# Products of h before the scan, Winograd values and queries, and a scan of four heads at once

## The chip, the cores and the metric

One core of one Trainium2 chip runs the kernel. The metric is the device time of one execution in microseconds, lower is better. The kernel before was run three times: 1786.86, 1792.22 and 1791.27 us, median 1791.27 us.

## The reference, cut to what matters

One residual block on 1024 tokens of 1024 features, all in float32. The part that the change touches is the gated linear attention of branch A:

```python
h = rms_norm(x, pre_mix_norm)
proj = h @ w_in        # q 4x128, k 4x128, v 4x256, gate 4x256, decay 16, c_q 384, c_kv 256, k_pe 64
q = h_q * 128 ** -0.5
log_a = log_sigmoid(h_a @ w_a2 + b_a2) / 16
b = cumsum(log_a, over the 64 tokens of a chunk)
k_dec = k * exp(b_end - b)
def step(state, chunk):
    state = exp(b_end) * state + k_dec.T @ v      # 128 x 256 per head
    out = q @ state
o = rms_norm(o, gla_norm) * silu(h_g)
...
mixed = (g_a * (o @ w_o_gla) + g_b * (attention @ w_o_mla)) @ w_out
x = x + rms_norm(mixed)
x = x + rms_norm(swiglu(rms_norm(x)))
```

Branch B is latent attention of eight heads from c_q, c_kv and k_pe; its code is not changed.

## The kernel before, in words

Activations lie transposed, feature on partitions and token along the row, in eight feature tiles (k tiles) of 128 x 1024. Every float32 operand of a product is split into a high and a low part: ACT rounds the high part (L104, or an activation of its own), DVE subtracts it to give the low part (L105), and `mm3` (L96) issues three matmuls for one product. Many large products take the seven-product form of Strassen and Winograd on 2 x 2 blocks (function `wino`): blocks b11, b21, b22 of the activations and the sums t1 to t4, and sums s1 to s4 of the weights, give seven block products of 12 matmuls each per row block in place of eight. `early1` computes the two products on b11 and b21 before the other operands exist, keeps one of them in DRAM (p1D) and reads it back later; `HPRE` is the number of groups treated so.

The order of the work is the order in which the Python code emits it, with a scheduler of the framework moving instructions of one engine past each other. Generators of side work (`run`, `back`) are advanced a piece at a time. SP issues all DMAs.

- 0 to 52 us: each k tile of x arrives, is split, and 24 matmuls make keys from it (p_k, eight psum banks).
- 52 to 92 us: decay input and rotary key (p_ha), the norm, h = x * gain * 1/rms (L351) with both token halves of all eight tiles split (hn), the plain product of the first head's queries (p_q) and of one latent tile (p_c).
- 92 to 137 us: values of head 0 (`v_proj`, p_v, 256-column matmuls, hn x wv), with `decays()` between the pieces: per token tile, p_z (decay logits), three ACT functions and one DVE step (L395), p_rv and p_tot (sums over a chunk), exp, and the decayed key kF (L410). It ends with four transposes (p_decp).
- 137 to 366 us: for each of the four heads, `gla_scan(hd)` with the next head's values as fill (for the last head, early products p_pre). Decayed keys are masked to two zero-padded copies (kdm, even and odd chunk) and so are queries (qm), so that all matmuls span 128 rows. Per token tile the state is updated (p_kv, st L734), split (sh, sl) and multiplied with q (p_o); the output is normed (rpow on POOL, L176), transposed (p_oT) and stored (oD). `down_sums` (L622 to L625) makes the 48 sums of blocks of the down projection's weights here, on DVE.
- 366 to 582 us: the other products of the 14 groups on h (`hrest`, p_wa and p_wb): latents, branch gates, output gates; `og_use` multiplies the gate with oD and stores ogD. The latents' norms run beside them (`side`).
- 582 to 842 us: preparation and latent attention of eight heads; from 842 us merge, output product, feed-forward.

Of the kernel before, what the change touches and what calls it, by code (L numbers as in the profile page):

```python
# [23 lines left out]
P = 128  # L24
# [37 lines left out]
HPRE = 14  # L62


def body(tc, a, out):
# [89 lines left out]
    def back(n=1):  # L155
        """emit n pieces of background work"""
# [21 lines left out]
    def norm(sq, dim, box, want_tok=None):  # L178
        """sq [128, 512]: squares summed over feature tiles; box gets 1/rms on every partition."""
# [24 lines left out]
    oD = dp.tile([8, P, 1024], F32, name="oD")  # L204
# [8 lines left out]
    hnD = dp.tile([8, P, 1024], F32, name="hnD")  # L213
# [80 lines left out]
    for kt in range(KD):  # L294
# [26 lines left out]
        else:  # L321
            back()
    rtok = cp.tile([P, NT], F32, name="rtok")
# [8 lines left out]
    # ---- decay input and rotary key (rows 0-63: key, 64-79 and 96-111: decay input)  # L332
# [11 lines left out]
    back(10)  # L344

# [1 line left out]
    hn = []  # L347
    for kt in range(KD):
        t = xs[kt]
        for j in range(2):  # L350
            dve.scalar_tensor_tensor(t[:, HS[j]], t[:, HS[j]], g(G_PRE + kt), rb[j], op0=ALU.mult, op1=ALU.mult)  # L351
        hn.append([])
# [5 lines left out]
        if kt == 1:  # L358
            hsb = U([P, 2, H2], name="hsb")
            act.copy(hsb, hps)  # L360

    haS = U([P, 1024], F32R, "haS")
# [6 lines left out]
    dma(krD, kraw[0:64])  # L369
    act.activation(haS[64:128], hat[64:128], AF.Identity, bias=gn[64:128, G_ONE:G_ONE + 1])  # L370
# [10 lines left out]
    def decays():  # L381
# [3 lines left out]
        for t in range(NT + 1):  # L385
# [12 lines left out]
            if prev is not None:  # L398
                u, (ph, pl) = t - 1, prev
                # sums over the rest of a chunk, and over each chunk (rows 2u and 2u + 1)  # L400
# [9 lines left out]
                dve.scalar_tensor_tensor(kf, kf, rtok[:, u:u + 1], e, op0=ALU.mult, op1=ALU.mult)  # L410
# [11 lines left out]
    # Winograd's form of Strassen's product on 2 x 2 blocks (K halves, token halves, tile pairs):  # L422
    # seven block products in place of eight.  Block (i, k) of the result is tile i, token half k.
    def op4(srcs, name):
        """[128, 512] blocks -> operand parts"""
        res = []
        for s in srcs:
            hl = U([P, 2, H2], F32R, name)
            split(s, hl[:, 0], hl[:, 1])
            res.append((hl[:, 0], hl[:, 1]))  # L430
        return res
# [8 lines left out]
    def wino(ops, slot, groups, npre):  # L440
        """groups: (weights, first tile, second tile, consumer).  Two steps: early() gives the first npre
        groups' products on b11 and b21 piece by piece; rest(side) all others, with side() called between
        the products."""
# [19 lines left out]
        pend = []       # (operand, product) with the operand's split emitted  # L463
# [120 lines left out]
    def t_ops(ops, b11, b12, b21, b22):  # L584
        """the operands from differences, from the float32 blocks (overwritten) of one pair of k tiles"""
        t3 = Hf("t3")
        dve.tensor_tensor(t3, b22, b12, op=ALU.subtract)
        if len(ops["b22"]) < 4:
            ops["b22"] += op4([b22], "b22")
        yield 1  # L590
        dve.tensor_tensor(b12, b12, b11, op=ALU.subtract)      # T1 = B12 - B11
        dve.tensor_tensor(b22, b22, b12, op=ALU.subtract)      # T2 = B22 - T1
        ops["t2"] += op4([b22], "t2")
        ops["t3"] += op4([t3], "t3")
        ops["t1"] += op4([b12], "t1")
        dve.tensor_tensor(b21, b21, b22, op=ALU.subtract)      # -T4 = B21 - T2
        ops["t4"] += op4([b21], "t4")
        yield 1

# [15 lines left out]
    def down_sums():  # L615
        """the sums of blocks of the down projection's weights"""
        for p in range(4):
            for c in range(0, KH * P, H2):
# [3 lines left out]
                dve.tensor_tensor(a22, a21, a22, op=ALU.add)           # S1 = A21 + A22  # L622
                dve.tensor_tensor(a21, a11, a21, op=ALU.subtract)      # S3 = A11 - A21
                dve.tensor_tensor(a11, a22, a11, op=ALU.subtract)      # S2 = S1 - A11
                dve.tensor_tensor(a12, a12, a11, op=ALU.subtract)      # S4 = A12 - S2  # L625
# [33 lines left out]
    ws = [wload(a["wq"][0]), wload(a["wc"][2])]  # L659
    pss = [A(name="p_q"), A(name="p_c")]  # L660
    for kt in range(KD):
        for m in range(2):
            for j in range(2):
                mm3(pss[m][:, j], ws[m][kt], hn[kt][j], kt == 0, kt == KD - 1)
    for j in range(2):
        t = Hf("cr")
        act.copy(t, pss[1][:, j])  # L667
        dma(crD[2, j], t)
    run(dgen)

# [9 lines left out]
    # rotary key  # L680
# [824 lines left out]
```

## Time and profile before

| what | value |
|---|---|
| runs | 1786.86, 1792.22, 1791.27 us (median 1791.27) |
| span of the profiled execution, first to last instruction | 1789.7 us |
| PE busy | 1742.2 us |
| DVE busy | 1269.8 us |
| ACT busy | 811.3 us |
| POOL busy | 37.9 us |
| mean granted clock of PE | 0.993 |

The profiled execution is known by its span alone, 1.6 us under the median of the runs. PE's busy time is the union of its matmuls; matmuls overlap, so the time that one costs is the distance between two starts and not its own duration. A window of the profile gives the busy time of each engine between two times. Idle time of an engine counts only where another engine waits for it.

### The profile page before, as it was taken

How to read it: one execution, taken by the hardware profiler on the slowest of the kernel's cores; microseconds unless marked ns; L12 is line 12 of the kernel's file. 1: busy time of each engine (PE TensorE's matmuls, PEld its weight loads, DVE VectorE, ACT ScalarE, POOL GpSimd, SP SyncE). 2: the span in 40 equal slices, each digit the busy share in tenths (PEclk: the TensorE clock that was granted, in tenths of full speed). 3: DMA queues.
4: the chain of work that ended last, by engine and by line, in shares of the span. 5: the costliest groups of instructions: out<-in, count | busy, mean ns of one | idle time of the engine just before them, and what ended most of it. 6: DMA issues, size and time to landing. Idle time of an engine off the chain costs nothing.

```text
span 1789.7 us, 25279 instructions
## 1 busy us (share of the span) xinstructions
PE 1742.2 (97%) x8818; PEld 1468.0 (82%) x8818; DVE 1269.8 (71%) x2275; ACT 811.3 (45%) x1511; POOL 37.9 (2%) x49
## 2 busy tenths in 40 slices
PE   8999999999999999999999999999999999999997
PEld 7889997777778898998878788787877788878886
DVE  7666666765766787787697567687787866755666
ACT  5485545633434554555442545452322233454552
POOL 0100000000000000000000000000000000000001
PEclk9999999999999999999999999999999999999998
DMA  6326676865576211112588653645454532593656
GB/s 213 129 80 197 192 235 223 276 200 184 195 238 222 67 45 49 35 51 95 169 302 284 207 191 129 240 140 177 165 183 141 182 101 97 182 312 116 195 176 215
DMA packets 172592, 305.50 MB, mean 171 GB/s; under 512 B 20080, under 2 KB 39280, under 8 KB 172464
## 3 DMA queue, kind: packets, MB, share of 16 engines
q1 hardware_dynamic: 172464, 303.88, 51.6%
q8 instruction: 69, 1.13, 0.3%
q14 instruction: 59, 0.48, 0.1%
HBM read 212.32 MB, written 89.39 MB: 169 GB/s over the span
## 4 chain that ended last, share of the span: by engine, by line
PE 74%; DMA 10%; DVE 9%; issue 3%; ACT 3%; SPq 1%; POOL 0%; DVEq 0%; ACTq 0%; POOLq 0%
PE p_wb L96 13%; PE p_wfd L96 10%; PE p_wa L96 9%; PE p_pre L96 6%; PE p_v L96 5%; PE p_wog L96 5%; PE p_wout L96 5%; PE p_sc L96 4%; PE p_av L96 3%; PE p_k L96 3%; DMA raw<-in_wfg_dram 2%; PE p_wqn L96 2%; DMA raw<-in_wgate_dram 1%; PE p_pt L1013 1%; DMA cl<-crD 1%
## 5 line engine op out<-in xcount | busy, mean ns | idle before, releaser
L104 ACT CAST wh<-raw 128x512 fp32r<-128x512 f32 (+1 forms) x335 | 200.2, 603 | 367.2 <-PE p_wfd L96 79.7
L105 DVE TENSOR_TENSOR wl<-raw,wh 128x512 fp32r<-128x512 f32 (+1 forms) x335 | 219.7, 663 | 153.8 <-ACT wh L104 142.8
L96 PE MATMUL p_wa<-t,wh 128*128 128x512 f32 x640 | 203.1, 397 | 5.0 <-DVE u L520 4.8
L96 PE MATMUL p_wb<-t,wh 128*128 128x512 f32 x640 | 198.1, 390 | 0.0
L96 PE MATMUL p_wfd<-ld,wh 128*128 128x512 f32 (+1 forms) x660 | 192.8, 376 | 2.3 <-ACT raw L1411 1.4
L96 PEld LDWEIGHTS p_wa<-t,wh 128*128 128x128 f32 x640 | 119.9, 190 | 35.5 <-DVE u L520 9.9
L96 PEld LDWEIGHTS p_wfd<-ld,wh 128*128 128x128 f32 x660 | 120.7, 188 | 26.1 <-ACT raw L1411 1.8
L96 PEld LDWEIGHTS p_wb<-t,wh 128*128 128x128 f32 x640 | 120.5, 188 | 25.1
L96 PE MATMUL p_wa<-t,wl 128*128 128x512 f32 x320 | 125.3, 393 | 0.0
L96 PE MATMUL p_wb<-t,wl 128*128 128x512 f32 x320 | 124.5, 389 | 0.0
L96 PE MATMUL p_wfd<-ld,wl 128*128 128x512 f32 (+1 forms) x330 | 123.1, 375 | 0.0
L104 ACT CAST wh<-sa 128x512 fp32r<-128x512 f32 x80 | 48.6, 620 | 149.3 <-DVE sa L458 90.4
L96 PE MATMUL p_v<-wh,hn 128*128 128x256 f32 x512 | 98.2, 283 | 0.7 <-ACT cr L667 0.6
L104 ACT CAST wh<-sb 128x512 fp32r<-128x512 f32 x80 | 49.7, 621 | 92.7 <-PE p_wb L96 47.5
L96 PEld LDWEIGHTS p_v<-wh,hn 128*128 128x128 f32 x512 | 82.3, 191 | 3.5 <-ACT cr L667 1.0
L96 PE MATMUL p_wog<-ld,wh 128*128 128x512 f32 x256 | 80.4, 392 | 1.0 <-DVE ld L105 0.7
L96 PE MATMUL p_pre<-b,wh 128*128 128x512 f32 x256 | 79.3, 396 | 0.0
L105 DVE TENSOR_TENSOR ld<-ld,ld 128x512 fp32r<-128x512 f32 x109 | 70.5, 686 | 11.3 <-ACT ld L104 10.9
L104 ACT CAST ld<-ld 128x512 fp32r<-128x512 f32 x109 | 63.5, 619 | 22.2 <-DMA ld<-fD 7.6
L96 PE MATMUL p_v<-wl,hn 128*128 128x256 f32 x256 | 72.4, 283 | 0.5 <-DVE wl L105 0.5
L96 PEld LDWEIGHTS p_wa<-t,wl 128*128 128x128 f32 x320 | 60.8, 190 | 13.1
L96 PEld LDWEIGHTS p_wfd<-ld,wl 128*128 128x128 f32 x330 | 62.1, 188 | 11.2
(349 smaller groups left out, 4076.4 us busy)
## 6 DMA issues: line engine op xcount, KB each, us to landing
ld<-fD SPq DMA_DIRECT2D x77, 256.0 KB, 4.1
raw<-in_wfd_dram SPq DMA_DIRECT2D x60, 256.0 KB, 2.8
raw<-in_wfg_dram SPq DMA_DIRECT2D x60, 256.0 KB, 3.6
raw<-in_wfu_dram SPq DMA_DIRECT2D x60, 256.0 KB, 3.0
raw<-in_wgate_dram SPq DMA_DIRECT2D x48, 256.0 KB, 3.3
fD<-sg SPq DMA_DIRECT2D x41, 256.0 KB, 2.0
p1D<-p SPq DMA_DIRECT2D x34, 256.0 KB, 3.0
p<-p1D SPq DMA_DIRECT2D x34, 256.0 KB, 3.9
```

The costliest lines, as they stand in the source:

```text
L96: pe.matmul(o, l, r, start=start, stop=stop, skip_group_check=skip)
L104: act.copy(h, src)
L105: dve.tensor_tensor(l, src, h.bitcast(F32), op=ALU.subtract)
L1013: pe.transpose(tp[:, jj, i * P:(i + 1) * P], prs[i][:, j * P:(j + 1) * P], ident)
```

## The change

- Values of all heads are made before the scan, in the seven-product form with 512-column matmuls (`v_gen`), and stored to DRAM (vD). The sums of the weights' blocks are made by POOL (`v_sums`, 16 operations of 128 x 512) while the keys are computed, from 16 loads of wv, and stored (svD).
- Queries of all heads are two more groups of `wino`, stored to qD; the output gates are stored as sgD and multiplied in the scan. `HPRE` falls from 14 to 6, the groups rise from 14 to 16.
- The latent tile p_c is computed from the split x right after p_ha and scaled later. The first query product is gone.
- h: only the first token half of each tile is split (hb); the second half goes straight into the sums t1 to t4 (`h_ops`, `t_ops`), with two of the four sums (t3 and b21) on POOL. The store and reload of h (hnD, `spilled_ops`) go.
- Decayed keys are split once (ACT kh, POOL kl) and stored to kdD, eight times.
- The scan runs after `hrest`, all four heads together: for each token tile two steps (a pair of heads each). An update is a matmul of 64 rows (the chunk's own tokens) in place of 128 zero-padded rows. The low part of the state is one 128 x 1024 operation per step, on DVE for the first pair and on POOL for the second (8 each). The preparation of the first attention heads (`pair_prep(0)`) is its fill.
- `down_sums` moves to POOL and is advanced during attention.

```diff
-HPRE = 14
+HPRE = 6
+        if kt >= 2:
+            run(vsum)
...
-        for j in range(2):
-            hl = U([P, 2, H2], F32R, "hn")
-            split(t[:, HS[j]], hl[:, 0], hl[:, 1])
-            hn[kt].append((hl[:, 0], hl[:, 1]))
-        dma(hnD[kt], t)
+    def t_ops(ops, b11, b12, b21, b22, alt=dve):
+        t3 = Hf("t3")
+        alt.tensor_tensor(t3, b22, b12, op=ALU.subtract)
...
+        dve.tensor_tensor(b12, b12, b11, op=ALU.subtract)
+        dve.tensor_tensor(b22, b22, b12, op=ALU.subtract)
...
+        alt.tensor_tensor(b21, b21, b22, op=ALU.subtract)
...
-                dve.scalar_tensor_tensor(kf, kf, rtok[:, u:u + 1], e, op0=ALU.mult, op1=ALU.mult)
+                dve.scalar_tensor_tensor(e, kf, rtok[:, u:u + 1], e, op0=ALU.mult, op1=ALU.mult)
+                kh, kl = Hf("kh", F32R), Hf("kl", F32R)
+                act.copy(kh, e)
+                pool.tensor_tensor(kl, e, kh.bitcast(F32), op=ALU.subtract)
+                dma(kdD[0, u], kh.bitcast(F32))
+                dma(kdD[1, u], kl.bitcast(F32))
...
-                dve.tensor_tensor(a22, a21, a22, op=ALU.add)           # S1 = A21 + A22
+                pool.tensor_tensor(a22, a21, a22, op=ALU.add)
...
+    vgen = v_gen()
+    for _ in range(9):
+        run(vgen)
         run(dgen)
-    for _ in range(4):
-        run(hpre)
+        run(hgen)
+    for _ in hpre:
+        run(hgen)
         run(dgen)
...
+                    for e in range(2):
+                        rsl = slice(64 * e, 64 * e + 64)
+                        mm(kv[:, e, hh], kd[t][x][rsl, hd * P:(hd + 1) * P], v[t][y][rsl, hd * DV:(hd + 1) * DV], n == 0, n == 2)
...
+            act.copy(sh, s2)
+            (pool if pr else dve).tensor_tensor(sl, s2, sh.bitcast(F32), op=ALU.subtract)
...
+    fill = pair_prep(0)
+    for n, _ in enumerate(gla_scan()):
+        if n >= 3:
+            run(fill)
```

The order of SP's queue in the first stage. Before, loads alone (x of one k tile, then weights):

```order
L298 DMA x_225<-in_xT_dram 128x1024
L110 DMA raw_694<-in_wq_dram 128x512
L110 DMA raw_700<-in_wc_dram 128x512
L110 DMA raw_706<-in_wc_dram 128x512
L298 DMA x_276<-in_xT_dram 128x1024
```

Now (x_236 and x_295 are the fourth and fifth k tile, vs the blocks of the values' weights):

```order
L323 DMA x_236<-in_xT_dram 128x1024
L309 DMA svD<-vs_231 128x512
L309 DMA svD<-vs_228 128x512
L309 DMA svD<-vs_230 128x512
L309 DMA svD<-vs_229 128x512
L323 DMA x_295<-in_xT_dram 128x1024
```

Four stores of sums that POOL makes now stand ahead of a load of x; the same holds once more, ahead of the load of the seventh k tile.

The end of the decays on PE. Before, products of the values (p_v) stand between the decays' last steps and up to their transposes:

```order
L96 MATMUL p_v_1388<-wh_1378,hn_632 128x256
L96 MATMUL p_v_1613<-wh_1366,hn_597 128x256
L96 MATMUL p_v_1613<-wl_1367,hn_597 128x256
L96 MATMUL p_v_1613<-wh_1366,hn_597 128x256
L96 MATMUL p_v_1613<-wh_1366,hn_606 128x256
L96 MATMUL p_v_1613<-wl_1367,hn_606 128x256
L418 MATMUL p_decp_1254<-cst,tot_1248 128x16 x4
```

Now:

```order
L96 MATMUL p_v_784<-wh_1149,hb_780 128x512
L96 MATMUL p_rv_1131<-lh_1066,rev 128x512
L96 MATMUL p_tot_804<-lh_1066,rev 16x512
L96 MATMUL p_rv_1131<-ll_1067,rev 128x512
L96 MATMUL p_tot_804<-ll_1067,rev 16x512
L96 MATMUL p_z_1165<-wh_752,haS_731 128x512
L96 MATMUL p_z_1165<-wl_753,haS_731 128x512
L96 MATMUL p_rv_1179<-lh_1127,rev 128x512
```

The last of the values' first two products stands ahead of the last three decay steps, which follow each other with no product between, then the transposes, and behind them everything else.

POOL and DVE in the same stage, now. POOL (x_98 and x_295 are the first and the fifth k tile of h):

```order
L483 TENSOR_TENSOR kl_862<-e_858,kh_861 128x512
L394 TENSOR_TENSOR t_185_867<-x_295,x_98 128x512
L403 TENSOR_TENSOR x_295<-x_295 128x512
L483 TENSOR_TENSOR kl_913<-e_909,kh_912 128x512
L483 TENSOR_TENSOR kl_974<-e_970,kh_973 128x512
```

DVE:

```order
L480 SCALAR_TENSOR_TENSOR e_858<-kF_542,rtok,e_858 128x512
L398 TENSOR_TENSOR x_98<-x_98 128x512
L399 TENSOR_TENSOR x_295<-x_295,x_98 128x512
L105 TENSOR_TENSOR wl_1264<-raw_1253,wh_1263 128x512
L465 SCALAR_TENSOR_TENSOR h_895<-p_z_890,h_893 128x512
```

DVE's L398 overwrites a block that POOL's L394 reads, and L394 stands behind the low part kl of a key whose decayed form DVE has only just made (L480). Before, POOL had no work of this kind in the stage.

## Rows read from the trace of the kernel before

**Rows 1.** Page, part 1: busy time, share of the span, instructions per engine.
```profile
PE 1742.2 (97%) x8818; PEld 1468.0 (82%) x8818; DVE 1269.8 (71%) x2275; ACT 811.3 (45%) x1511; POOL 37.9 (2%) x49
```

**Rows 2.** Windows by stage: length, busy (instructions) of PE, PEld, DVE, ACT, POOL; clock; DMA.
```profile
69.50:91.00 21.50, 21.50 (x96) 17.65 (x95) 20.92 (x33) 12.59 (x21) 5.36 (x8) 1.00 0.52 183
...
92.00:137.50 45.50, 44.41 (x292) 38.77 (x293) 29.21 (x46) 34.54 (x63) 0.00 (x0) 1.00 0.28 87
137.50:366.00 228.50, 224.80 (x1445) 201.63 (x1444) 156.21 (x286) 124.60 (x273) 12.07 (x16) 1.00 0.68 224
366.00:582.00 216.00, 207.66 (x916) 169.29 (x916) 142.69 (x227) 86.94 (x137) 4.79 (x4) 0.98 0.63 207
598.00:842.00 244.00, 240.82 (x1528) 216.94 (x1526) 190.47 (x493) 129.56 (x285) 0.00 (x0) 1.00 0.16 49
```

**Rows 3.** Timeline of PE: start, us, form; 256 and 512 columns.
```profile
153.34 0.28 PE L96 MATMUL p_v<-wh,hn 128*128 128x256 f32 x1
153.46 0.28 PE L96 MATMUL p_v<-wl,hn 128*128 128x256 f32 x1
...
1442.66 0.62 PE L96 MATMUL p_wb<-b,wh 128*128 128x512 f32 x2
...
1443.34 0.39 PE L96 MATMUL p_wb<-b,wh 128*128 128x512 f32 x1
```

**Rows 4.** PE's groups by form: instructions, busy us, mean ns.
```profile
L96 PE MATMUL p_v<-wh,hn 128*128 128x256 f32 x512 | 98.2, 283 | 0.7 <-ACT cr L667 0.6 <-ACT wh L104 0.2
...
L96 PE MATMUL p_q<-hn,wh 128*128 128x512 f32 x128 | 40.3, 395 | 0.4 <-DVE vl L105 0.4
...
L96 PE MATMUL p_kv<-vh,kdm 128*128 128x256 f32 x128 | 28.7, 289 | 0.0
```

**Rows 5.** Timeline of PE: transposes of 16 rows, next product.
```profile
129.29 0.41 PE L418 MATMUL p_decp<-cst,tot 16*128 16x16 f32 x4
129.63 0.74 PE L96 MATMUL p_pre<-hn,wh 128*128 128x512 f32 x2
```

**Rows 6.** Waits of PE in 366 to 582 us: total, times, longest.
```profile
PE p_wa L96 <- DVE u L520: 3.4, 2, 2.9
PE p_nrm L96 <- DVE cl L643: 2.9, 2, 2.2
```

**Rows 7.** Windows: first and last of three stretches of lower clock; one late product group.
```profile
378.00:382.00 4.00, 4.00 (x16) 3.16 (x15) 1.51 (x3) 0.62 (x1) 0.00 (x0) 0.81 0.61 196
510.00:514.00 4.00, 4.00 (x13) 3.14 (x12) 2.58 (x5) 1.34 (x2) 0.00 (x0) 0.67 0.70 242
1444.19:1463.45 19.26, 19.26 (x85) 15.69 (x85) 15.15 (x24) 6.49 (x12) 0.00 (x0) 1.00 0.46 151
```

**Rows 8.** POOL's groups by form.
```profile
L1400 POOL TENSOR_TENSOR raw<-raw,xr 128x256 f32<-128x256 f32 x6 | 4.4, 730 | 10.3 <-DVE raw L1399 8.5 <-DMA xr<-x1D 1.8
...
L714 POOL MEMSET kdm<- 64x1024 f32 x2 | 1.9, 951 | 2.8 <-DMA hnD<-x 2.7
L716 POOL MEMSET qm<- 128x512 f32 x2 | 1.1, 530 | 3.5 <-DMA hnD<-x 2.3 <-DVE hn L105 1.2
```

**Rows 9.** Waits of ACT in 0 to 52 us.
```profile
ACT xh L305 <- DMA x<-in_xT_dram: 10.5, 8, 2.7
```

**Rows 10.** Timeline of DVE: scaling and split of h.
```profile
63.40 2.07 DVE L351 SCALAR_TENSOR_TENSOR x<-x,gn,rb 128x512 f32<-128x512 f32 x3
...
66.65 1.28 DVE L105 TENSOR_TENSOR hn<-x,hn 128x512 fp32r<-128x512 f32 x2
```

**Rows 11.** Timeline near the end, DVE with POOL idle, then both.
```profile
1783.95 0.41 DVE L1400 TENSOR_TENSOR raw<-raw,xr 128x256 f32<-128x256 f32 x1
...
1784.67 0.90 DVE L1400 TENSOR_TENSOR raw<-raw,xr 128x256 f32<-128x256 f32 x1
...
1784.57 0.72 POOL L1400 TENSOR_TENSOR raw<-raw,xr 128x256 f32<-128x256 f32 x1 [1.22 <-DMA xr<-x1D]
```

**Rows 12.** DVE's groups by form, state of the scan.
```profile
L734 DVE SCALAR_TENSOR_TENSOR st<-st,dec,p_kv 128x256 f32<-128x256 f32 x60 | 28.4, 474 | 9.0 <-PE p_kv L96 8.4
```

More of the change, by code (lines that the diff above doesn't have):

```diff
@@ L203, in body @@
     krD = dp.tile([64, 1024], F32, name="krD")
-    oD = dp.tile([8, P, 1024], F32, name="oD")
+    qD = dp.tile([HEADS_A, P, 1024], F32, name="qD")
+    kdD = dp.tile([2, NT, P, H2], F32, name="kdD")
+    vD = dp.tile([2, NT, P, 1024], F32, name="vD")
+    svD = dp.tile([4, 4, P, H2], F32, name="svD")
+    sgD = dp.tile([8, P, 1024], F32, name="sgD")
     ogD = dp.tile([8, P, 1024], F32, name="ogD")
@@ L658, in body @@
     dgen = decays()
[L659 to L669, printed above, removed]
     def rot_tables():
@@ L807, in body, with v_use, v_gen, halves @@
-    hops = dict(b11=[t[0] for t in hn[:4]], b21=[t[0] for t in hn[4:]], b22=[t[1] for t in hn[4:]],
-                t1=[], t2=[], t3=[], t4=[])
-    def lat_use(m0, m1):
+    def v_use(i, t, src):
+        h, l = Hf("vh", F32R), Hf("vl", F32R)
+        split(src, h, l)
+        for n, x in enumerate((h, l)):
+            dma(vD[n, 4 * (i % 2) + t][:, HS[i // 2]], x.bitcast(F32))
+    def v_gen():
+        def halves():
+            t = [U([P, 2, H2], name="vu") for _ in range(2)]
+            return [t[n // 2][:, n % 2] for n in range(4)]
+        def prod(src, bop, bank, first):
+            for k in range(4):
+                w = wop(wraw(src(k)))
+                for t in range(4):
+                    mm3(bank[t], cols(bop[k], slice(t * P, (t + 1) * P)), w, first and k == 0, k == 3, not first)
+                yield 1
+        def raw(i, j):
+            return lambda k: v_block(i, j, k)
+        def summed(n):
+            return lambda k: svD[n, k]
+        x = [A(name="p_v") for _ in range(2)]
+        x = [x[t // 2][:, t % 2] for t in range(4)]
+        yield from prod(raw(0, 0), hops["b11"], x, True)
+        p1 = halves()
+        for t in range(4):
+            act.copy(p1[t], x[t])
+        yield from prod(raw(0, 1), hops["b21"], x, False)
+        for t in range(4):
+            v_use(0, t, x[t])
+        yield 1
+        y = [B(name="p_v") for _ in range(4)]
+        u2 = halves()
+        yield from prod(summed(1), hops["t2"], y, True)
+        for t in range(4):
+            dve.tensor_tensor(u2[t], y[t], p1[t], op=ALU.add)
+        yield from prod(summed(2), hops["t3"], y, False)
+        for t in range(4):
+            dve.tensor_tensor(p1[t], y[t], p1[t], op=ALU.add)
+        yield from prod(summed(0), hops["t1"], x, True)
+        for t in range(4):
+            c = Hf("c22")
+            dve.tensor_tensor(c, x[t], p1[t], op=ALU.add)
+            v_use(3, t, c)
+        yield from prod(raw(1, 1), hops["t4"], y, True)
+        for t in range(4):
+            dve.tensor_tensor(p1[t], y[t], p1[t], op=ALU.add)
+            v_use(2, t, p1[t])
+        yield from prod(summed(3), hops["b22"], x, False)
+        for t in range(4):
+            dve.tensor_tensor(u2[t], x[t], u2[t], op=ALU.add)
+            v_use(1, t, u2[t])
+        yield 1
@@ L882, in body @@
-    back(100)
-    for _ in hpre:
-        finish(sgen)
-        run(ggen)
-    finish(ggen)
-    lgen = [x for i in range(2) for x in [latent_norm(i)]]
+    finish(vgen)
+    lgen = [latent_norm(i) for i in range(2)]
     def side(gi):
-        if gi >= 2 and gi % 2 == 0:
+        if gi >= 5 and lgen:
             while lgen and next(lgen[0], None) is None:
                 lgen.pop(0)
+        else:
+            back()
     hrest(side)
@@ new lines, in body, with gla_out @@
+    fill = pair_prep(0)
+    for n, _ in enumerate(gla_scan()):
+        if n >= 3:
+            run(fill)
+    finish(fill)
+    def gla_out(j, ogs, use):
+        for m in range(8):
+            w = wload(a["wog"][m])
+            ga = Hf("ga")
+            dma(ga, gaD[m][:, HS[j]])
+            ps = B(name="p_wog")
+            for kt in range(KD):
+                mm3(ps, w[kt], ogs[kt], kt == 0, kt == KD - 1)
+                if kt == 3:
+                    yield 1
+            dve.tensor_tensor(ga, ps, ga, op=ALU.mult)
+            use(m, ga)
+            yield 1
@@ L1049, in body @@
     gen = prep_all()
+    sums = down_sums()
     done = 0
@@ L1055, in body @@
             done = max(done, need[hd])
+        run(sums)
         cur = (hd, blk, qk(hd, blk))
```

330 lines of the change are left out of this document (154 added, 176 removed).

## Prediction

> **What bounds the kernel now.** The page's first part says PE: busy for 97% of the span, DVE for 71%, POOL for 2% [rows 1]. I therefore price each part of the change on PE first and then ask, stage by stage, whether DVE or POOL becomes the later one. The windows by stage show where there is slack [rows 2]: DVE is busy 29.2 of 45.5 us beside the decays, 156 of 228.5 in the scans, 143 of 216 in the rest of the products on h, 190 of 244 in attention; PE is idle only a few us in each. Busy PE is not PE at its pitch, so I compare with pitches: starts 0.12 us apart for 256 columns, and three matmuls of 512 columns in 0.68 us, 0.227 each [rows 3]. A change of less than 0.3% (5.4 us) can't be told from none here; with the median of 1791.3 "the same" is 1785.9 to 1796.7.
>
> **PE's savings.**
> Values: 512 + 256 matmuls of 256 columns [rows 4] at 0.12 are 92.2 us. The new form has 7 x 4 x 12 = 336 of 512 columns, 76.3 us: **-15.9**. Queries: 128 + 64 [rows 4] at 0.227 are 43.6; two groups of 84 are 38.1: **-5.5**. The latent tile costs the same in its new place.
> Updates: 128 + 64 of 256 columns [rows 4], 23 us. Two halves of 64 rows each can at best run side by side, which would save 11.5; at worst each costs what a full one did, 0. It counts only where PE bounds the scan, which I doubt below: **0**. The only row with few rows is four transposes of 16, and the next product begins 0.34 us after their start [rows 5]: 0.085 each, with 16 columns. It shows no stop of PE between the two forms.
> The scans' window: 942 matmuls of 256 columns at 0.12, 436 of 512 at 0.227 and 64 short ones at 0.11 make 219 us; it lasts 228.5 [rows 2], so 9.5 us go to small stalls where short products alternate. Products of h alone have few (about 2 for this content): **-7.4** (-9 to -5).
> The rest of the products on h: 852 matmuls of 512 columns and 64 short ones make 200.5 us; the window lasts 216 [rows 2], a loss of 15.5. PE waits for DVE [rows 6], and after each of three such waits its clock is low for a while: 4 us with 0.81 granted, later 4 us with 0.67 [rows 7], so part of it is spent at the lower of its two levels, 1.2 GHz. All 14 groups here have six products left and reload the seventh; a late group with all seven takes 19.26 us for 84 matmuls, 0.2 over its pitch [rows 7]. Of 16 groups now 10 are whole, and the latents' norms, which make one of those waits [rows 6], keep to later groups: loss 6 instead of 15.5, **-10** (-14 to -5).
>
> **What comes on top.**
> Keys: four stores of svD stand ahead of the fifth k tile's load in SP's queue, four more ahead of the seventh's. Each group waits for four additions on POOL. Price of one: POOL took 730 ns for 128 x 256 [rows 8]; its fills take 530 for 512 columns and 951 for 1024, so the fixed part is 0.11 and 512 columns should cost about 1.35 (between 0.73 and 1.46). Four are 5.4 us, just what 24 matmuls of one k tile last (5.45). ACT already waits for x in this stage, 10.5 us in all [rows 9], so a late x is late on PE. Bounds: 0, if POOL keeps up, and 2 x 5.4; I take the middle, **+5**.
>
> Decays: the stage that I think decides. DVE starts scaling at 63.40, at 0.665 us per piece and 0.61 per split [rows 10]. By the changed order, 90 DVE operations stand up to the last decayed key: 32 with a scalar, 57 without, one wide: 21.3 + 34.5 + 1.2 = 57.0 us. So DVE alone ends at 120.4. PE has p_ha, then p_c (the 96 matmuls of 69.5 to 91 us were p_q and p_c [rows 2]; p_c's 48 are 10.9 us, to 80.4), then 96 matmuls of the values' first two products and 48 of the decays, 32.7 us: it ends at 113.1. Behind it nothing but the last decay steps may run. That is 7 us of wait with DVE undisturbed. But POOL has 19 operations there (sums, kl, t3, b21), 25.7 us. The trace has one place where the two meet: a DVE addition of two SBUF operands takes 0.41 us alone and 0.90 when it starts 0.1 us into one of POOL's of 0.72, both ending within 0.3 us [rows 11]: DVE stood still until POOL was through. The Trainium skill ("SBUF — State Buffer", section "Who interferes with whom") states this as an exclusive lock for DVE instructions with two SBUF inputs beside a GpSimd instruction that reads SBUF; by it all 57 plain operations are exposed, and the trace's one meeting agrees. Besides, DVE's L398 must wait for POOL's t3, which stands behind a kl that waits for ACT: some 3 us each, four times. All of POOL's time in DVE's way would be +33, none of it +4 to +7. I take half of POOL's 25.7: **+20** (+4 to +30).
>
> Scan: DVE has 60 state updates of 474 ns [rows 12], 0.394 from start to start (neighbours overlap by some 0.08, as the three scalings of 0.74 that take 2.07 [rows 10]), 4 copies, 16 low parts of q, 32 gated outputs of the same size, 8 low parts of 1024 columns at 1.15, 26 preparation steps at 0.605, 16 tiny ones: 69.5 us. PE has 58 to 69 (updates 11.5 or 23, outputs 23, transposes 7, preparation 16). Before, this content lay under 219 us of other products. POOL has 8 low parts at 2.59 (a 1024-column price by the same line) and five groups of `down_sums`, 45 us; every second state waits for its low part on POOL, behind a group of sums of up to 5.4 us. DVE operations with two SBUF operands (50 of them) meet it half the time: about 12 us. With 3 us to fill the chain the scan ends after 84.5 against the 69.1 that the same matmuls cost before: **+15.5** (0 to +28).
>
> Attention: the rest of the sums on POOL, beside 78% of DVE busy [rows 2], PE waiting for DVE's operands already: **+3** (0 to +8). DVE loses 27 us of sums from the scans, where it was not the bound: 0. Stores and reloads (qD, vD, sgD, kdD instead of hnD, oD) lie in stages with DMA at 0.16 to 0.68 [rows 2]: 0, and if the reload of a tile comes late in the scan it is inside that range.
>
> **Sum.** -15.9 - 5.5 - 7.4 - 10 + 5 + 20 + 15.5 + 3 = +4.7 us, on a profiled span of 1789.7 (1.6 under the median of the runs): 1794.4, or **1796** as a median. The 38.8 us that PE saves are given back where POOL and DVE stand in one another's way.
>
> **Rivals.**
> *A: POOL's work falls into DVE's gaps.* DVE has a third of every stage free, and one meeting in the trace is little evidence. Then the decays cost +4 and the scan +3: 1796 - 16 - 12.5 = **1768**. It decides by the decays' transposes: before 125 us for A, after 135 for the forecast.
> *B: slower, the lock in full.* If each of POOL's operations stops DVE, and the low part of each second state waits behind a group of sums: keys +9, decays +30, scan +28, attention +8, together 31.5 over the forecast: **1827**. It decides from the point at which more than three quarters of POOL's time shows up as longer DVE operations.
> *C: the halves of 64 rows do not run side by side*, so that this part does not do what it says. The 16-row transposes speak for a price per matmul that few rows don't lower. Updates then cost 23 us: nothing while DVE bounds the scan; where PE bounds it, +11.5, **1806** with the rest as forecast. The Trainium skill ("TensorEngine Tiling (Array Packing)", section "Key Properties") says that a change of tiling mode drains TensorE; with 32 changes in the scan a stop would go on top, but the row of the transposes shows none of 0.1 us, so I add nothing.
>
> **How the numbers follow.** Forecast 0.44, its own range 1784 to 1808 (the decays at 13 or 27, the scan at 8 or 22); A 0.30 (1755 to 1782), because POOL's time is only 80 us in stages where DVE has some 180 free; B 0.20 (1812 to 1840); C as the deciding part 0.06. The range leaves out about the lower tenth (most of A's better half below 1760) and the upper tenth (B above 1824): **1760 to 1824**. Faster by over 0.3%: A and 0.04 of the forecast, 0.34. Same: 0.26, a good half of the forecast. Slower: the rest of it, B and C, 0.40.
>
> **What would show it.** Right: PE's matmuls fall by 456 (432 of the values, 24 of the queries); a gap on PE of 10 to 25 us in front of p_decp, put down to DVE or ACT steps of the decays; subtractions on DVE of 1 us and more where POOL is busy; a scan stage of 80 to 90 us with DVE over 80% busy; the rest of h at 0.23 us per matmul. Wrong: p_decp before 125 us; DVE's mean for a 128 x 512 subtraction still 0.69; a scan of 70 us with PE at its pitch; or a gap in the key stage of more than 10 us.

## The result, and the profile after

| | time |
|---|---|
| before, 4 runs | 1791.62 us median (1786.86 to 1792.22) |
| after, 4 runs | 1901.84 us median (1900.62 to 1904.92) |
| ratio | 1.0618, 95% interval 1.0596 to 1.0641 |

110 us slower; 1796 was forecast, with a range up to 1824. The profiled execution of the changed kernel has a span of 1898.6 us. The page's first part and its row of the granted clock, which answer to [rows 1]:

```profile
PE 1758.5 (93%) x8362; PEld 1451.3 (76%) x8362; DVE 1281.4 (67%) x2249; ACT 810.0 (43%) x1495; POOL 160.6 (8%) x133
...
PEclk9987999999976879999999999999999999999998
```

PE has 456 matmuls fewer, as the change says, and yet more busy time (1758.5 for 1742.2 us): in two stretches of the clock's row, the decays (slices 3 and 4) and the scan (12 to 15), the granted clock is below nine tenths. POOL went from 38 to 161 us.

To see where the 110 us lie, I cut both traces at the same events of PE: first p_v, p_decp, last product on h, end of the latent attention (last p_av). After (window, its length, then PE, PEld, DVE, ACT, POOL busy with instructions, clock, DMA share, GB/s; the third window ends at the scan's last transposes and the fourth goes on to the last p_av):

```profile
87.20:160.00 72.80, 41.68 (x146) 27.47 (x144) 50.15 (x75) 48.48 (x88) 17.52 (x14) 0.77 0.37 131
160.00:548.10 388.10, 377.74 (x1652) 306.53 (x1652) 222.37 (x345) 156.15 (x253) 16.98 (x15) 0.99 0.50 165
548.10:706.00 157.90, 99.64 (x558) 81.90 (x557) 79.74 (x166) 57.99 (x148) 60.59 (x48) 0.71 0.76 244
706.00:989.60 283.60, 278.16 (x1729) 248.73 (x1728) 219.47 (x544) 147.23 (x320) 24.92 (x20) 1.00 0.30 95
989.60:1898.60 909.00, 886.23 (x3965) 725.31 (x3963) 644.01 (x1037) 359.10 (x632) 12.37 (x13) 0.99 0.57 188
```

Before, with the scans inside the second window:

```profile
92.40:129.30 36.90, 36.21 (x255) 32.11 (x255) 23.98 (x37) 31.55 (x56) 0.00 (x0) 1.00 0.19 57
129.30:581.40 452.10, 440.06 (x2395) 377.06 (x2394) 303.64 (x520) 213.75 (x413) 16.86 (x20) 0.99 0.66 216
581.40:880.30 298.90, 295.00 (x1837) 264.72 (x1836) 231.56 (x574) 156.47 (x337) 0.00 (x0) 1.00 0.20 62
880.30:1789.70 909.40, 885.17 (x3965) 724.06 (x3963) 644.29 (x1037) 358.70 (x632) 11.95 (x13) 0.99 0.57 188
```

| stage | before | forecast | after |
|---|---|---|---|
| start to first p_v | 92.4 | 85.4 | 87.2 |
| first p_v to p_decp | 36.9 | 52.7 | 72.8 |
| p_decp to the last product on h | 452.1 | 377 | 388.1 |
| last product on h to last p_av | 298.9 | 370 | 441.5 |
| the rest | 909.4 | 909 | 909.0 |

The forecast column is the prediction's sum written by these events (p_c's end at 80.4 and the 5 us of the keys; for the products on h, what the other rows leave of 1794.4). Its error of 104 us has four parts: the start +2, decays +20, products on h +11, and the stage with the scan **+71**. The scan itself, 548 to 706 us, has PE busy for 99.6 of 157.9 us, and that at a clock of 0.71; DVE, which was to be its bound, is busy for half of it. So no engine's throughput sets it. What PE waits for there (total, times, longest):

```profile
PE p_o L96 <- ACT sh L970: 19.9, 14, 4.3
PE p_kv L96 <- DMA vh<-vD: 16.2, 3, 12.1
PE p_o L96 <- POOL sl L971: 5.5, 6, 1.8
PE p_kv L96 <- DVE st L966: 4.7, 4, 2.0
```

One step of the scan, all engines in order of time (start, duration, engine, line, operation, idle time before it and what ended that):

```profile
604.81 0.69 DVE L886 TENSOR_TENSOR qr<-p_qp,cos 128x512 f32<-128x512 f32 x1
605.42 0.47 DVE L966 SCALAR_TENSOR_TENSOR st<-st,dec,p_kv 128x256 f32<-128x256 f32 x1
...
605.80 0.68 DVE L887 TENSOR_TENSOR qr<-qr,qt 128x512 f32<-128x512 f32 x1
...
606.41 0.48 DVE L966 SCALAR_TENSOR_TENSOR st<-st,dec,p_kv 128x256 f32<-128x256 f32 x1
...
607.17 0.69 DVE L891 TENSOR_TENSOR ql<-qr,qs 128x512 fp32r<-128x512 f32 x1
...
608.57 0.99 DVE L966 SCALAR_TENSOR_TENSOR st<-st,dec,p_kv 128x256 f32<-128x256 f32 x2
...
609.59 1.04 ACT L970 CAST sh<-st 128x1024 fp32r<-128x1024 f32 x1 [2.45 <-DVE st L966]
...
610.69 0.58 PE L96 MATMUL p_o<-sh,qm 128*128 128x256 f32 x1 [4.30 <-ACT sh L970]
610.71 2.35 POOL L971 TENSOR_TENSOR sl<-st,sh 128x1024 fp32r<-128x1024 f32 x1 [10.40 <-ACT sh L970]
...
612.21 0.88 DVE L983 TENSOR_SCALAR ty<-ty 128x2 f32<-128x2 f32 x1
...
613.11 0.58 PE L96 MATMUL p_o<-sl,qm 128*128 128x256 f32 x1 [1.84 <-POOL sl L971]
...
613.16 0.70 POOL L176 TENSOR_TENSOR ty<-ty,mhalf 128x2 f32<-128x2 f32 x1
```

This is one round. DVE updates the state in four operations; a sum (L887), a copy and a split (L891) of the attention's preparation and two gated outputs stand between them, so the last two start 3.2 us after the first. ACT rounds the state (1.04), PE starts its output with the rounded part after 4.30 us of waiting; POOL needs 2.35 for the low part, PE waits 1.84 more. At 612.21 DVE's operation on 128 x 2 elements takes 0.88 us; the median of its 16 in the scan is 0.17. It ends with POOL's: DVE had to wait for POOL. Five of the 16 start well inside an operation of POOL's (598.79, 612.21, 636.60, 659.32 and 686.59 us); they take 0.35 to 0.88 us and all end within 0.03 us of it. The Trainium skill ("SBUF — State Buffer", section "Who interferes with whom") says that tensor_scalar can contend with GpSimd when its operands meet the conditions of a mode that uses both ports; this row agrees.

### The profile page after: what moved, and what is told of

Same layout as the page of the kernel before. It is cut to its first block, busy times and chain, and to the rows that moved or that the text cites. A ratio compares the mean times of both kernels' runs of the same rounds, so it can differ in the third digit from the quotient of the medians.

```text
span 1898.6 us, 24642 instructions
## 1 busy us (share of the span) xinstructions
PE 1758.5 (93%) x8362; PEld 1451.3 (76%) x8362; DVE 1281.4 (67%) x2249; ACT 810.0 (43%) x1495; POOL 160.6 (8%) x133
## 4 chain that ended last, share of the span: by engine, by line
PE 51%; DVE 5%; DMA 5%; issue 2%; POOL 1%; ACT 1%; SPq 0%; DVEq 0%; ACTq 0%; POOLq 0%
PE p_wfd L96 10%; PE p_wb L96 10%; PE p_wa L96 6%; PE p_wout L96 5%; PE p_sc L96 4%; PE p_pre L96 4%; PE p_wog L96 3%; PE p_av L96 3%; DMA raw<-in_wfg_dram 2%; PE p_wqn L96 2%; PE p_pt L1078 1%; PE p_wkn L96 1%; PE p_v L96 1%; PE p_qp L96 1%; DMA ld<-omD 1%
## 5 line engine op out<-in xcount | busy, mean ns | idle before, releaser
L104 ACT CAST wh<-raw 128x512 fp32r<-128x512 f32 (+1 forms) x345 | 207.1, 603 | 392.2 <-PE p_wfd L96 84.7
L105 DVE TENSOR_TENSOR wl<-raw,wh 128x512 fp32r<-128x512 f32 (+1 forms) x345 | 231.0, 674 | 183.2 <-ACT wh L104 179.2
L96 PE MATMUL p_wb<-t,wh 128*128 128x512 f32 x672 | 208.9, 390 | 3.9 <-DVE u L592 2.9
L96 PE MATMUL p_wa<-t,wh 128*128 128x512 f32 x672 | 211.4, 394 | 1.1 <-DVE u L584 0.9
L96 PEld LDWEIGHTS p_wa<-t,wh 128*128 128x128 f32 x672 | 124.7, 188 | 32.8 <-DVE u L584 4.2
L96 PEld LDWEIGHTS p_wb<-t,wh 128*128 128x128 f32 x672 | 125.6, 188 | 30.8 <-issue 3.3
L176 POOL TENSOR_TENSOR ty<-ty,mhalf 128x2 f32<-128x2 f32 (+1 forms) x27 | 24.1, 891 | 1354.0 <-DVE ty L186 1283.7
L96 PE MATMUL p_wa<-t,wl 128*128 128x512 f32 x336 | 131.2, 391 | 0.0
L96 PE MATMUL p_wb<-t,wl 128*128 128x512 f32 x336 | 130.8, 389 | 0.0
L96 PEld LDWEIGHTS p_wb<-t,wl 128*128 128x128 f32 x336 | 63.1, 188 | 13.2
L96 PE MATMUL p_wa<-b,wh 128*128 128x512 f32 x216 | 68.0, 396 | 3.8 <-DVE c L603 3.7
```

What stands on the lines that cost most here:

```text
L96: pe.matmul(o, l, r, start=start, stop=stop, skip_group_check=skip)
L104: act.copy(h, src)
L105: dve.tensor_tensor(l, src, h.bitcast(F32), op=ALU.subtract)
L176: pool.tensor_tensor(dst, src, mhalf.broadcast_to([P, n]), op=ALU.pow)
```

## The experiments

Sixteen kernels; ratios are to the kernel before on the same chip (changed kernel: 1.0618). Lengths are from the traces, in us: D from the first p_v to p_decp, S from the first p_kv to the last p_oT, A from the last product on h to the last p_av.

| run | time | ratio (95%) | D | S | A |
|---|---|---|---|---|---|
| changed kernel | 1901.8 | 1.0618 (1.0596 to 1.0641) | 72.8 | 144.9 | 441.5 |
| e1 sums to DVE, ahead of the scan | 1898.9 | 1.0565 (1.0534 to 1.0596) | 73.5 | 133.6 | 426.8 |
| e2 decays without POOL | 1891.6 | 1.0524 (1.0494 to 1.0555) | 67.8 | 143.4 | 439.7 |
| e3 states' low parts on DVE | 1896.8 | 1.0553 (1.0522 to 1.0584) | 73.3 | 139.4 | 436.0 |
| e4 updates two steps ahead | 1881.9 | 1.0470 (1.0440 to 1.0501) | 72.7 | 124.7 | 421.6 |
| e5 e1 to e4, v_sums on DVE | 1867.3 | 1.0410 (1.0351 to 1.0469) | 61.4 | 113.0 | 404.8 |
| e6 idle work for PE | 1902.8 | 1.0608 (1.0551 to 1.0665) | 74.0 | 142.0 | 438.1 |
| e9 no norm in the scan | 1893.5 | 1.0550 (1.0465 to 1.0634) | 72.8 | 135.0 | 429.0 |
| e10 loads left out | 1893.9 | 1.0552 (1.0465 to 1.0639) | 73.5 | 140.9 | 436.9 |
| e11 products between decay steps | 1890.8 | 1.0535 (1.0446 to 1.0624) | 84.1 | 145.0 | 441.5 |
| e12 e5, e11, later scaling | 1862.3 | 1.0376 (1.0292 to 1.0459) | 75.8 | 112.2 | 405.1 |
| e13 outputs from the first state | 1881.1 | 1.0457 (1.0308 to 1.0607) | 74.6 | 108.0 | 419.1 |
| e14 e13 with loads left out | 1886.8 | 1.0489 (1.0332 to 1.0646) | 74.3 | 109.1 | 426.1 |
| e15 sums of h behind the decays | 1894.3 | 1.0531 (1.0373 to 1.0688) | 61.9 | 144.9 | 440.4 |
| e16 e5 and e15 | 1860.8 | 1.0344 (1.0176 to 1.0513) | 57.9 | 114.4 | 407.6 |
| e7 before, 64-row halves | 1804.4 | 1.0056 (1.0036 to 1.0076) | | | |
| e8 before, scans bare | 1822.5 | 1.0160 (1.0103 to 1.0218) | | | |

The intervals are wide against single effects of 5 to 15 us, so I read the stages. Each is from one trace; where an edit doesn't touch a stage, its length differs by about 2 us between traces (D 72.7 to 74.6, S 143.4 to 145.0).

**One cause at a time, e1 to e4.**

```diff
-                pool.tensor_tensor(a22, a21, a22, op=ALU.add)
+                dve.tensor_tensor(a22, a21, a22, op=ALU.add)
...
+        if nside[0] % 4 == 2:
+            run(sums)
```

> The sums for the down projection go from POOL (spread over scan and attention) to DVE, inside the products on h before the scan, where DVE is busy half the time. Theory Q (the sums' loads, stores and buffers in SP's queue hold the scan's own loads): the scan stage, 548 to 706 us in the changed kernel, becomes at least 50 us shorter and the time falls to 1850 or below. Rival L (the latency of a scan step with too little other work beside it): at most 20 us shorter, 1880 to 1895.

S fell by 11, A by 15; nearly all of it came back in the products on h, which are now 14 us longer (402.4). Theory Q fell.

```diff
-                pool.tensor_tensor(kl, e, kh.bitcast(F32), op=ALU.subtract)
+                dve.tensor_tensor(kl, e, kh.bitcast(F32), op=ALU.subtract)
...
-            yield from t_ops(hops, *[...], pool)
+            yield from t_ops(hops, *[...])
```

> In the decays only: the low parts of the decayed keys and the two sums t3 and b21 on DVE in place of POOL. If the hand-overs between POOL and DVE make the gap ahead of the decays' transposes (they start at 160.0 us), it closes by 10 to 20 us, and the time falls as much, 1882 to 1892. If the chain of one token tile through ACT, DVE and PE makes it, the transposes stay within 5 us of 160 and the time within 5 of 1902.

D fell by 5, and the transposes start at 153.5, 6.5 us earlier: between the two cases. The time fell by 10.

```diff
-            (pool if pr else dve).tensor_tensor(sl, s2, sh.bitcast(F32), op=ALU.subtract)
+            dve.tensor_tensor(sl, s2, sh.bitcast(F32), op=ALU.subtract)
```

> All low parts of the state on DVE (1.2 us) in place of every second on POOL (2.36 us each). If POOL's place in the chain makes the scan long: 20 us or more off. Theory L: a step's chain is 1.2 us shorter in every second step of 16, 10 to 15 us off at most. Theory Q: within 5 us of 1902, since the loads come no earlier.

S fell by 5.5: POOL's place in the round counts for little.

```diff
-            nxt = update(*steps[n + 1]) if n + 1 < len(steps) else None
-            late.append((t, pr, *output(t, pr, *cur)))
+            if n + 2 < len(steps):
+                curs.append(update(*steps[n + 2]))
+            late.append((t, pr, *output(t, pr, *curs.pop(0))))
...
```

> Updates run two steps ahead of the outputs in place of one, loads one step earlier; nothing else. Theory L: PE has a step's more work to fill its waits, its waits in the scan (60 us) halve, the clock stays up, 40 us or more off: 1860 or below. Theory Q: the loads stand in the same queue behind the same stores, at most 10 us off.

S fell by 20, half of what theory L expected: the largest single effect so far, got without less work or fewer loads.

**Together, and the clock, e5 and e6.** e5 joins the four edits and one more, the sums of the values' weights (first of its four lines):

```diff
-            pool.tensor_tensor(a22, a21, a22, op=ALU.add)
+            dve.tensor_tensor(a22, a21, a22, op=ALU.add)
...
```

> The changed kernel with all of POOL's new work taken back by DVE (sums of the values' weights, t3, b21, keys' low parts, states' low parts, the down projection's sums inside the products on h) and updates two steps ahead. If POOL's work and its hand-overs are the cause of the 110 us, the time falls to within 15 us of the kernel before (by the single edits so far, 8 to 25 us each, they sum to some 55 to 60 us). Theory L (a scan with nothing beside it costs more than its work): the scan stage from the last product on h to the last p_oT stays over 100 us and the time over 1840.

With POOL's new work gone, A is still 106 us longer than before (404.8 against 298.9). POOL was a part of it, not the cause.

```diff
+            dm = B(name="p_dm")
+            for _ in range(8):
+                mm(dm, cn[0][0][:, 0:P], cn[1][0][:, HS[0]], True, True)
             late.append((t, pr, *output(t, pr, *cur)))
```

> The changed kernel with 8 more matmuls of 512 columns in each of 16 scan steps, whose result nobody reads, in PE's program ahead of the step's outputs: 128 x 0.227 = 29 us more work. If the low clock after PE's waits makes the scan long, the clock there rises from about 0.75 to over 0.9 and the time does not grow, perhaps falls by up to 20. If PE's throughput or the loads bound the scan, the time grows by 20 to 29 us.

The scan's stage of e6, to be read against the window 548.10:706.00 above:

```profile
551.60:707.00 155.40, 114.13 (x686) 92.14 (x685) 83.11 (x166) 58.47 (x148) 61.27 (x48) 0.87 0.79 249
```

128 more matmuls, the clock at 0.87 in place of 0.71, and the stage is 155.4 us in place of 157.9. PE's waits and the low clock belong together: what PE does there costs nothing as long as it falls into the round. But the round's length did not shrink with the better clock either.

**The kernel before, e7 and e8.**

```diff
...
-            for e in range(2):
-                mm3(kv[:, e], (kdm[e][0][:, t], kdm[e][1][:, t]), v, True, True)
+            for n, (x, y) in enumerate(((0, 0), (0, 1), (1, 0))):
+                for e in range(2):
+                    rsl = slice(64 * e, 64 * e + 64)
+                    mm(kv[:, e], kds[x][rsl, t], v[y][rsl], n == 0, n == 2)
...
```

> The kernel before with one part of the change alone: updates on 64-row halves (no zero-padded keys), its psum tile from the pool of two-bank tiles, the values' psum in one-bank tiles. If halves run side by side, PE saves 96 x 0.12 = 11.5 us in a stage that PE bounds, and the time falls by 8 to 14 us. If not, it stays within 5 us of the kernel before.

It is 10 us slower. Timeline of PE around one update in e7 (x2 is a pair of halves):

```profile
193.43 0.28 PE L96 MATMUL p_v<-wh,hn 128*128 128x256 f32 x1
193.64 0.39 PE L96 MATMUL p_kv<-vh,kdm 64*128 64x256 f32 x2
193.86 0.28 PE L96 MATMUL p_kv<-vl,kdm 64*128 64x256 f32 x2
193.98 0.28 PE L96 MATMUL p_kv<-vh,kdm 64*128 64x256 f32 x2
194.19 0.39 PE L96 MATMUL p_o<-sh,qm 128*128 128x256 f32 x1
```

The same in the kernel before, first matmul of an update and first of the output behind it:

```profile
195.21 0.28 PE L96 MATMUL p_kv<-vh,kdm 128*128 128x256 f32 x1
...
195.93 0.28 PE L96 MATMUL p_o<-sh,qm 128*128 128x256 f32 x1
```

The pairs do run side by side: 0.12 from one to the next, what one full matmul took. But the first pair starts 0.21 after the last full matmul, where 0.12 is usual, the second pair 0.22 after the first, and the output again 0.21 after the last pair: 0.28 us per update for the two changes. Three pairs take 0.55 and their entry 0.09 more, against 0.72: 0.08 us saved for 0.36 hoped for, 2.6 us in 32 updates. The Trainium skill ("TensorEngine Tiling (Array Packing)", section "Key Properties") says that a change of tiling mode drains TensorE; this trace shows 0.09 to 0.10 us lost on either side of the changes, which agrees, and which I had ruled out from a row of transposes. A wait of 5.6 us of p_kv and 5 us more in the products on h eat the rest. Whether the other psum pools of e7 made the wait was not tried, and why the products on h grew stays open.

```diff
         sgen = gla_scan(hd, vs[hd])
+        if hd + 1 < HEADS_A:
+            finish(fill)
```

> The kernel before with the scans of the first three heads laid bare: the next head's values are computed ahead of a scan and not beside it. Same work, no load added. Theory L: each bare scan pays its chain, with PE waiting and a lower clock; a step costs about 5 us more than the 1.5 of its matmuls, 24 steps: 60 to 120 us longer than before. Theory Q (loads, queues): no loads here, so within 15 us of the kernel before.

28 us longer: more than theory Q allows, less than I gave theory L. Waits of PE from 128 to 395 us, and the windows of the three bare scans:

```profile
PE p_o L96 <- ACT sh L104: 12.7, 13, 2.1
PE p_oT L764 <- ACT osc L755: 6.6, 8, 1.4
```

```profile
160.60:187.00 26.40, 18.68 (x109) 16.07 (x108) 24.22 (x50) 15.09 (x39) 2.84 (x3) 0.87 0.71 230
222.20:246.50 24.30, 17.44 (x108) 14.95 (x107) 21.55 (x46) 13.81 (x37) 2.83 (x3) 0.86 0.65 211
281.60:304.30 22.70, 14.98 (x100) 12.36 (x99) 19.67 (x42) 13.89 (x37) 2.46 (x3) 1.00 0.56 183
```

A bare scan of one head lasts 23 to 26 us, and PE waits for the same pair as after the change (sh) and for the norm (osc), 12.7 and 6.6 us of some 24 in all. But DVE, which also makes the down projection's sums here, is busy for 24.2 of the 26.4 us, 21.6 of 24.3 and 19.7 of 22.7. So this run shows that a scan without cover costs time; it can't tell the round from DVE's throughput.

**The round taken apart, e9, e10, e13, e14.**

```diff
-                act.activation(osc[:, i], op[:, i], AF.Square, accum_out=ss[:, i:i + 1])
-            dve.tensor_scalar(ss, ss, 1.0 / DV, EPS, op0=ALU.mult, op1=ALU.add)
-            rpow(rr, ss, 2)
-            for i in range(2):
-                act.activation(osc[:, i], op[:, i], AF.Copy, scale=rr[:, i:i + 1])
+                act.activation(osc[:, i], op[:, i], AF.Copy, scale=0.5)
```

> The changed kernel without the norm inside the scan (the squares, the sums' scaling on DVE, the power on POOL are left out; the outputs are scaled by a constant). In the trace, ACT's rounding of the next state stands behind the scaling that waits for POOL's power, so each step is one round through PE, ACT, DVE, POOL, ACT, DVE, PE. If that round sets the step (9.1 us each), a step falls to 6 us or less and the scan by 40 us or more: 1865 or below. If the loads set it: less than 15 us off.

S fell by 10.

```diff
+            if t >= 2:
+                kd[t], v[t] = kd[t - 2], v[t - 2]
...
-            for i in range(2):
+            for i in range(2 if t < 2 else 0):
                 dma(kd[t][i].bitcast(F32), kdD[i, t])
```

> The changed kernel with the scan's loads of values and keys left out from the third token tile on (the first two tiles' are used again; 6 x 1.5 MB less). If loads behind a busy queue set the step, the scan falls by 40 us or more: 1865 or below. If the round through the engines sets it: 5 to 15 us off (PE's waits for vh and vl after the first are about 8 us).

S fell by 4. The loads of keys and values after the first two tiles are not the cause, and neither is the norm alone.

```diff
-            late.append((t, pr, *output(t, pr, *cur)))
+            late.append((t, pr, *output(t, pr, *first)))
```

> The changed kernel, all work and loads kept, but every output product takes the first step's state (sh, sl) in place of its own: PE no longer waits for the state's low part in any step. If the round PE, DVE, ACT, DVE or POOL, PE of a step sets the scan (145 us from the first p_kv to the last p_oT), it falls by 35 us or more, towards the 73 to 85 that DVE's work takes; if loads or the norm's round set it, by less than 15.

S fell by 37, with all work and loads kept. The stage of e13 up to its last transposes:

```profile
549.90:672.00 122.10, 80.87 (x551) 68.01 (x551) 71.88 (x156) 54.46 (x144) 42.73 (x36) 0.83 0.86 274
```

So it is shown that the outputs' wait for their own state, and not an amount of work, makes 37 us of S. The granted clock rose with it, 0.71 to 0.83. But A fell by 22 only; some 14 us came back, nearly all of it behind the scan's last transposes:

```profile
672.00:969.00 297.00, 283.92 (x1737) 252.78 (x1736) 225.54 (x554) 149.71 (x323) 42.36 (x33) 0.97 0.35 110
```

The changed kernel needs 283.6 us for this part, with 24.9 us of POOL's work in it for 42.4 here. That the sums pushed behind the scan make the difference was not tried.

e14 is e13 with the edit of e10.

> The same with the loads of values and keys left out from the third tile on as well. If loads and the state's round share the cost (each hides behind the other when one alone is taken away), the scan falls by 50 us or more, to 95 or below; if the first edit fell short and this one too, what is left is the norm's round and PE's clock.

S stayed at 109, so the loads left out are not hidden behind the round. S is still some 39 us longer than the 69.5 us of DVE's work. One place of this trace where time is lost (all engines):

```profile
610.82 1.28 POOL L672 TENSOR_TENSOR raw<-raw,raw 128x512 f32<-128x512 f32 x1
...
612.04 0.72 POOL L176 TENSOR_TENSOR ty<-ty,mhalf 128x2 f32<-128x2 f32 x1
...
612.79 0.47 ACT L989 ACTIVATE osc<-p_o,ty 128x256 f32<-128x256 f32 x1 [5.98 <-POOL ty L176]
...
614.55 2.37 DVE L950 SCALAR_TENSOR_TENSOR qm<-qt,qm 128x256 fp32r<-128x256 f32 x1 [6.06 <-ACT qm L949]
...
615.24 0.79 PE L96 MATMUL p_wqn<-cnh,wh 128*128 128x512 f32 x1 [3.45 <-ACT osc L989]
```

Three of the down projection's sums run ahead of the power ty in POOL's queue (from 608.11 us on; DVE had ty's operand ready at 608.05); ACT waits 5.98 us for ty with the scaling of an output at the head of its queue, and the next state's rounding and the next queries behind it; DVE waits 6.06 us for those queries; PE 3.45 for psum that ACT has not read. One operation of 0.72 us, late on the least busy engine, holds up the other three. How much of these 39 us such places make is not shown: e13 without POOL's sums was not tried, and in e5, which has none on POOL, S is 113.

**The decays, e11, e15, e16; the best of all, e12 and e16.**

```diff
-    for _ in range(9):
+    for i in range(9):
         run(vgen)
         run(dgen)
         run(hgen)
+        if i >= 2:
+            run(hpre)
```

> The changed kernel with one loop altered: the six early groups' products (144 matmuls, 33 us), which stood behind the decays, are emitted between the decay steps. If the 45 us that PE stands or runs at low clock ahead of p_decp are the decays' chain without cover, most of the products fit in: 20 to 30 us off, 1872 to 1882. If DVE's own work sets the stage (the products bring 12 more splits to it), p_decp moves later by as much and the time stays within 8 us.

p_decp came 11 us later, the products on h took 18 less: 7 us gained by the stages, 11 by the time: nearer the second case.

```diff
     for _ in range(9):
         run(vgen)
         run(dgen)
-        run(hgen)
```

> The changed kernel with the sums t1 to t4 of h made beside the early products, behind the decays, in place of between the decay steps. If DVE's queue (30 operations of these sums and the hand-overs to POOL, 4 x 3.3 us) delays the decays, the 72.8 us from the first p_v to p_decp shrink by 15 to 25, and the time by 12 to 25. If a tile's own chain sets it, by less than 8.

D fell by 11, and 5 of them came back in the products on h: between the two cases.

e12 is e5 with e11's edit, and the scaling of an output is emitted a step later:

```diff
+            o = (t, pr, *output(t, pr, *curs.pop(0)))
+            if mid:
+                late.append(scaled(*mid.pop(0)))
+            mid.append(o)
...
```

> All that helped, together: POOL's work back on DVE, two steps ahead, early products between the decay steps, and the scaling of an output one step later. By the sum of the single effects 1867 - 20 for the cover - 10 to 20 for the scaling: 1825 to 1845. It stays slower than the kernel before, since the scan still has little beside it; if it came within 10 us of 1792 the theory of the bare scan would be wrong.

1862.3: S as in e5 (112.2), so the later scaling brought nothing. e16 is e5 with e15's edit:

> The same order of the sums of h, with POOL's work back on DVE and updates two steps ahead: 1867 before this edit; 1845 to 1857 if the effects add. Still slower than the kernel before by over 50 us, since the scan stands alone.

e16 is the fastest version of the changed kernel (e12 is 1.5 us behind it, within the noise), still 62 us behind the kernel before on its chip. No version here beats the kernel before. A in e16 is 407.6 us against 298.9 and D 57.9 against 36.9, so what is missing lies in the scan that stands alone and, for the smaller part, in the decays; a version with the scan beside other products again, and the values in the seven-product form, was not tried: 28 of 34 four-kilobyte buffers hold the operands of h while those products run.

## Why the prediction was wrong

- **The scan** (forecast 84.5, with +15.5 in the sum; measured 157.9) is the step that failed. I priced it by DVE's throughput, 69.5 us, plus 12 for the lock and 3 "to fill the chain". DVE was busy for 79.7 us there, near the 69.5 with some lock; the count was right, the bound was not. What I left out is that an output needs its own state and that a state needs a round through PE, DVE, ACT, DVE or POOL, with one step of lead and 16 us of other products for cover: 9.1 us a step, where its work on the busiest engine is 4.3. In PE's program the updates after the next stand behind the outputs that wait. e13 shows it with -37 us of S and -22 of A, e4 with -20 of both; e8 agrees, but has DVE nearly full. Some 39 us of S over DVE's 69.5 are left in e13 and stay open. I had even written that "before, this content lay under 219 us of other products" (all products of that window, the scan's own 53 among them) and counted that as PE work that is no longer needed in small pieces, not as cover that is gone. The lock and POOL's queue, which I took as the rivals' mechanism, account for less: 11 us of S in e1, 5.5 in e3; the DVE operations in the scan that last longer beside POOL's than their like do so by some 6 us together, where I had put 12. Rival B had the right sign but not the mechanism: it asked for three quarters of POOL's time (60.6 us there) as longer DVE operations, and a tenth came.
- **The clock.** The forecast let PE wait at no further price. In the scan the granted clock is 0.71; 99.6 us of busy PE stand for some 70 at full clock (an estimate, 99.6 x 0.71). In e6 the clock is 0.87 and the stage as long, so what the low clock costs there was not shown.
- **The start of the scan.** 12.4 us pass between the last product on h and the first p_kv, waiting for vh; the forecast gave 3. SP issues the load of vh at 554.22 us, 6 us into this wait and behind eight loads of cos and sin, and the DMA share of the 12.4 us is 0.97. That it is due to buffers held until the last product ends was not tried.
- **The decays** (+20 forecast, +40 over PE's 32.7 us measured). Of the 20 us, 7 were DVE's own work as the bound and 13 POOL's time in DVE's way. Neither came so: DVE is busy for 50.2 of the 72.8 us, and three of its operations there are longer beside POOL's than their like, by 2.0 us together (a plain 128 x 512 operation takes 0.72 us in the mean, so my sign against the lock, a mean still at 0.69, all but came). What PE waits for is ACT, in the chain of a token tile:

```profile
PE p_rv L96 <- ACT lh L104: 20.5, 5, 5.2
PE p_decp L493 <- ACT tot L489: 9.5, 1, 9.5
```

The hand-over from POOL to DVE was as put, from the changed kernel's timeline:

```profile
105.08 0.74 DVE L480 SCALAR_TENSOR_TENSOR e<-kF,rtok,e 128x512 f32<-128x512 f32 x1
...
105.86 0.62 ACT L482 CAST kh<-e 128x512 fp32r<-128x512 f32 x1 [0.92 <-DVE e L480]
...
106.56 1.30 POOL L483 TENSOR_TENSOR kl<-e,kh 128x512 fp32r<-128x512 f32 x1 [21.84 <-ACT kh L482]
...
107.81 1.29 POOL L394 TENSOR_TENSOR t<-x,x 128x512 f32<-128x512 f32 x1
...
109.13 0.69 DVE L398 TENSOR_TENSOR x<-x 128x512 f32<-128x512 f32 x1 [3.30 <-POOL t L394]
```

L398 waits 3.30 us for t3, which stood behind kl, which waited for ACT; 12.2 us in four of them, as worked out. The lock shows too, ahead of this stage, at the sums of the values' weights:

```profile
80.03 1.28 POOL L305 TENSOR_TENSOR vs<-vs,vs 128x512 f32<-128x512 f32 x1
...
81.39 1.63 POOL L306 TENSOR_TENSOR vs<-vs,vs 128x512 f32<-128x512 f32 x1
...
81.88 1.69 DVE L433 TENSOR_TENSOR hat<-hsb,rb 64x512 f32<-64x512 f32 x1
```

DVE's 64 x 512 product starts inside one of POOL's and takes 1.69 us, 0.69 in the kernel before. But e2, without the hand-over, gains 5 us of D only, and e5, without the sums of the values' weights as well, has D at 61. e15 gains 11 by moving the sums of h away, and e16, with both, is at 57.9. The other 21 us over the kernel before would be the chain of a token tile through ACT, DVE and PE, which v products covered before; no run separates it, and e11, with products between the decay steps, made D longer.
- **Keys** (+5 forecast, +7.5 measured at the last p_k, 59.4 for 51.9): right in kind and size. With the sums on DVE (e5) p_k still ends at 59.2, so it is not POOL's time alone; whether the stores in SP's queue make the rest was not tried.
- **Products on h** (-17.4 forecast for stalls there and between the scans): 388.1 for 377 us. PE is idle for 10 of them, most of it in waits for DVE (the longest 2.9 us), as in the kernel before, so less of the stalls went than I had put.
- **Updates on halves** at 0: right in the changed kernel, where PE doesn't bound the scan; e7's pairs run side by side, so rival C is out. The sentence that the transposes show no stop between the two forms was wrong (e7).
- **Price of POOL's operations**: 1.35 us for 512 columns forecast, 1.27 undisturbed; 2.59 for 1024 columns, 2.36 measured. **The rest** of the program is unchanged, 909.0 for 909.4. Attention from its first to its last p_av takes 274.3 us, 271.9 before and 271.5 in e1, which takes the sums out of it: they cost 2 to 3 us, as forecast (+3).

## What to carry to other kernels

A recurrence is priced by the round that one step makes through the engines, divided by the steps that may overlap, and not by the busiest engine's work. Whoever takes independent products out of the shadow of such a recurrence has to count them as cover that is lost. An engine that is nearly idle is no free place for work if a short operation of a chain stands in the same queue: here a power of 0.7 us behind three sums held up three other engines.

## What had not been expected of the hardware

Going from matmuls of 128 rows to halves of 64 and back costs 0.28 us, while pairs of 64-row halves that write to two psum banks run at 0.12 us a pair. Eight more matmuls per step, 29 us of work at full clock, cost no time in a stage where PE waits, and raised the granted clock from 0.71 to 0.87. An operation of DVE's on 128 x 2 elements, 0.17 us alone, took up to 0.88 where it started inside one of POOL's, and ended with it.
